# Reordering the end of a hybrid decoder layer on eight Trainium2 cores: two interleaved column blocks, x added from SBUF with plain stores, and weight buffers freed head by head

## The chip, the cores and the metric

The kernel runs on the eight NeuronCores of one Trainium2 chip. Each core computes 2048 of the 16384 tokens, and no core talks to another. The metric is device time in microseconds of the slowest core. A program on all eight cores has two states: in some executions a few cores get a lower TensorE clock and the time is some per cent longer, whatever the kernel.

Engine names in the profile: PE is TensorE (matmuls), DVE is VectorE, ACT is ScalarE, POOL is GpSimd, SP is the sync engine. A trailing q (SPq, POOLq) is that engine's instruction queue.

## The reference, cut to what matters

Only the last step is touched by the change. y is the concatenation of three mixer branches A, B and C, 1024 channels each, already multiplied by its gates:

```python
g_a, g_b, g_c = split_cols(branch_norm[l], BRANCH_WIDTHS)
y = jnp.concatenate([rmsnorm(ya, g_a), rmsnorm(yb, g_b), rmsnorm(yc, g_c)], axis=-1)
out = jnp.einsum('bse,ed->bsd', y, w_out[l])      # (tokens x 3072) @ (3072 x 2048)
x = x + rmsnorm(out, norm_post[l])
```

## The kernel before: the parts that matter

y lies transposed in SBUF (channels on partitions), and w_out comes in 12 pieces of 1 MB in bfloat16 on arrival: four column blocks `db` of 512 columns times three branches `br`. The kernel has five buffers for these pieces and nine for finished rows, and does the 16 token tiles in two groups (`half`, 7 and 9 tiles), so all of w_out is read twice. For each tile, column block and branch, eight matmuls fill one PSUM bank (a "group" below, 1.71 us). ScalarE evicts branch 0, scaled by the branch's root-mean-square; VectorE adds branches 1 and 2; ScalarE squares the sum.

```python
def o_evict(half, db, i, br):
    ...
    if br == 0:    # ScalarE
        P.op("act", lambda e: e.activation(out=ra, in_=pv, func=AF.Identity, scale=sc(c)), ...)
    else:          # VectorE
        P.op("dve", lambda e: e.scalar_tensor_tensor(out=ra, in0=pv, scalar=sc(c), in1=ra, op0=ALU.mult, op1=ALU.add), ...)
    if br == 2:    # ScalarE: sum of squares of this column block
        P.op("act", lambda e: e.activation(out=asrow(i, psb(b)), in_=ra, func=AF.Square, accum_out=...), ...)
```

When all four column blocks of a tile are there, `final` multiplies the row and adds it to `out`, which already holds a copy of x (made by DMA much earlier). The addition is done by an accumulating DMA:

```python
def final(half, i):
    ...                                     # reduce_sum (DVE), sqrt (ACT), reciprocal (DVE)
    P.op("dve", lambda e: e.scalar_tensor_tensor(out=rf, in0=rf, scalar=sc(ST_FR + t), in1=asrow(i, gpost[:]),
                                                 op0=ALU.mult, op1=ALU.mult), ...)          # 128 x 2048
    P.op("pool", lambda e: e.dma_start(out=asrow(i, out_d[t * 128:(t + 1) * 128, :]), in_=rf,
                                       accum_op=ALU.add), reads=Mr, waits=xcp, dma_sem=f"d_out{i}")
```

The order of work: in each column block the first two and last two tiles go branch by branch, the tiles between them one after the other. The weight piece that comes five pieces later is loaded when the last tiles have used its buffer. Buffers 0 to 3 lie where the weights of branch B lay, so the first pieces wait for branch B. Tile rows of the second group reuse the SBUF of the first group's rows, and so must wait until those have been stored.

```python
for half in range(2):
    n = NT[half]                            # 7, 9
    for db in range(4):
        head, mid, tail = [0, 1], list(range(2, n - 2)), [n - 2, n - 1]
        ...                                 # head: by branch; mid: tile by tile; tail: by branch, load_wo(1) after each branch
        if db == 3: ...                     # final of a tile one unit after its last group, the last three at the end
```

## Time and profile before

| | before |
|---|---|
| time of the fast runs | 1366.8, 1367.25, 1367.4 us |
| PE busy, share of the span | 1243.3 us, 91% |
| last matmul to end of the program, core 0 | 36.8 us |
| PE waits in the output projection, core 0 | 1.9 (pool engine) + 4.7 (weights) + 7.1 us (weights) |

First the page of the kernel before: the span, and two rows of its 40 equal slices of 34 us each. A digit is the busy share of the slice in tenths (9 is 90% or more).

```profile
span 1366.8 us, 17431 instructions; the slowest of 8 cores (1359.3 to 1366.8 us)
PE   2686799999999999999999999999899997999990
DMA  9921129741299990303003411303254499825198
```

PE is full except at the beginning, which the change leaves alone, in slices 29 and 34, and in the last one.

The waits of PE from 960 us on (total, number of times, longest):

```profile
PE ps L364 <- DMA arena<-wst: 11.8, 2, 7.1
PE ps L510 <- POOL arena L503: 1.9, 1, 1.9
```

And the tail in the timeline (start, duration, engine, line, operation; in brackets the idle time before it and what ended that):

```profile
1319.69 10.31 PE L364 MATMUL ps<-arena 128*128 128x512 bf16 x47
1330.11 0.75 DVE L932 SCALAR_TENSOR_TENSOR arena<-ps,arena 128x512 f32<-128x512 f32 x1 [0.97 <-PE ps L364]
1332.28 2.35 DVE L950 SCALAR_TENSOR_TENSOR arena<-arena 128x2048 f32<-128x2048 f32 x1
1335.46 2.35 DVE L950 SCALAR_TENSOR_TENSOR arena<-arena 128x2048 f32<-128x2048 f32 x1
1338.63 2.35 DVE L950 SCALAR_TENSOR_TENSOR arena<-arena 128x2048 f32<-128x2048 f32 x1
1342.12 1.44 POOL L953 DMA_DIRECT2D out<-arena  x1 [1.85 <-issue]
```

L932 is the last eviction, 0.9 us after the last matmul. L950 is the multiply of `final`: three are left, one after the other. The last accumulating store is issued at 1342.1, but the program ends only at 1366.8: the stores issued earlier are still in the queue ahead of it.

### The profile page before, as it was taken

The page shows a single profiled execution, that of the slowest core. Times are in us where ns is not written, and L with a number is a line of the kernel's source. Part 1 is how long each engine was busy: PE and PEld are TensorE (multiplying, and loading weights), DVE is VectorE, ACT ScalarE, POOL GpSimd, SP SyncE. Part 2 cuts the span into 40 slices and gives each one's busy share as a digit, 9 for nine tenths or more (in the row PEclk, how much of TensorE's full clock was granted, in tenths as well). Part 3 has the DMA queues.
Part 4 walks back from the last instruction along what each step waited for, and adds up shares of the span by engine and source line. Part 5 has one row for each costly group of instructions (what it writes and reads, how often), then busy time and mean ns, then how long its engine had stood idle before and what let it go on. Part 6 is the DMA issues. An engine that isn't in the chain of part 4 may idle for free.

```text
span 1366.8 us, 17431 instructions; the slowest of 8 cores (1359.3 to 1366.8 us)
## 1 busy us (share of the span) xinstructions
PE 1243.3 (91%) x6242; PEld 575.8 (42%) x6242; DVE 533.5 (39%) x868; ACT 431.2 (32%) x781; POOL 126.4 (9%) x165
## 2 busy tenths in 40 slices
PE   2686799999999999999999999999899997999990
PEld 0232345544444444444444444444434443444440
DVE  3646564435544433443222223322322254223362
ACT  2254332122245555553322222222222222222220
POOL 1000021110101010101001010101100011000011
PEclk7798899999999999999999999999999999999995
DMA  9921129741299990303003411303254499825198
GB/s 243 252 81 62 62 43 168 122 67 34 32 182 158 166 166 9 63 1 62 1 0 50 75 28 35 63 1 62 53 85 82 89 153 154 137 50 93 32 152 125
DMA packets 25284, 119.38 MB, mean 87 GB/s; under 512 B 2672, under 2 KB 4976, under 8 KB 20720
## 3 DMA queue, kind: packets, MB, share of 16 engines
q0 software_dynamic: 21136, 80.22, 36.2%
q1 hardware_dynamic: 4064, 38.05, 11.9%
q8 instruction: 51, 0.84, 0.3%
q14 instruction: 33, 0.27, 0.1%
HBM read 164.93 MB, written 33.55 MB: 145 GB/s over the span
## 4 chain that ended last, share of the span: by engine, by line
PE 82%; DVE 6%; DMA 5%; ACT 2%; issue 2%; POOL 0%; DVEq 0%; SPq 0%; ACTq 0%; POOLq 0%
PE ps L364 81%; DMA arena<-wst 3%; DVE arena L439 2%; DMA arena<-xT 2%; DVE arena L420 1%; ACT arena L430 1%; DVE arena L950 1%; DVE arena L531 1%; DVE arena L473 1%; PE ps L700 1%; PE ps L510 0%; DVE arena L537 0%; ACT arena L499 0%; ACT arena L464 0%; DVE arena L577 0%
## 5 line engine op out<-in xcount | busy, mean ns | idle before, releaser
L364 PE MATMUL ps<-arena 128*128 128x512 bf16 (+3 forms) x5922 | 1236.9, 370 | 79.1 <-ACT arena L430 53.6
L364 PEld LDWEIGHTS ps<-arena 128*128 128x128 bf16 x5922 | 561.6, 98 | 730.9 <-issue 122.5
L496 ACT ACTIVATE arena<-arena 128x512 bf16<-128x512 f32 x96 | 68.8, 716 | 398.2 <-DVE arena L839 173.2
L932 DVE SCALAR_TENSOR_TENSOR arena<-ps,arena 128x512 f32<-128x512 f32 x128 | 95.9, 751 | 201.0 <-PE ps L364 181.1
L503 POOL TENSOR_TENSOR arena<-arena 128x512 bf16<-128x512 bf16 x48 | 55.1, 1148 | 730.2 <-ACT arena L499 636.4
L936 ACT ACTIVATE ps<-arena 128x512 f32<-128x512 f32 x64 | 38.5, 601 | 223.8 <-DVE arena L932 186.2
L531 DVE TENSOR_TENSOR arena<-arena 128x512 f32<-128x512 f32 (+5 forms) x80 | 64.3, 803 | 77.7 <-ACT arena L525 72.7
L371 POOL DMA_DIRECT2D arena<-wst x96 | 56.5, 607 | 393.1 <-PE ps L364 375.8
L833 DVE SCALAR_TENSOR_TENSOR arena<-ps,arena 128x512 f32<-128x512 f32 x32 | 24.1, 752 | 154.7 <-PE ps L364 83.3
L647 DVE CAST arena<-ps 128x512 bf16<-128x512 f32 x32 | 22.1, 692 | 101.6 <-PE ps L364 98.8
L499 ACT ACTIVATE arena<-arena 128x512 bf16<-128x512 f32 x96 | 58.8, 613 | 0.0
L929 ACT ACTIVATE arena<-ps,arena 128x512 f32<-128x512 f32 x64 | 43.3, 683 | 25.4 <-PE ps L364 11.7
L776 DVE BATCH_NORM_STATS2 arena<-ps 128x6 f32<-128x512 f32 x32 | 22.4, 699 | 73.0 <-PE ps L364 70.2
L517 ACT ACTIVATE arena<-ps 128x512 f32<-128x512 f32 x64 | 36.3, 596 | 40.0 <-PE ps L364 39.6
L439 DVE SCALAR_TENSOR_TENSOR arena<-arena 128x512 bf16<-128x512 f32 x64 | 42.8, 745 | 0.4
L420 DVE RECIPROCAL arena<-arena 128x512 f32<-128x512 f32 (+2 forms) x6 | 15.4, 2570 | 67.3 <-ACT arena L418 43.5
L950 DVE SCALAR_TENSOR_TENSOR arena<-arena 128x2048 f32<-128x2048 f32 x16 | 37.6, 2351 | 1.7
L525 ACT COPY arena<-ps 128x512 f32<-128x512 f32 x32 | 18.5, 578 | 60.0 <-PE ps L510 53.5
L430 ACT ACTIVATE arena<-arena 128x2048 bf16<-128x2048 f32 x16 | 30.0, 1905 | 8.4 <-DMA arena<-xT 7.5
L675 ACT ACTIVATE ps<-ps,arena 128x256 f32<-128x256 f32 x64 | 28.5, 446 | 3.1
L793 ACT ACTIVATE arena<-ps,arena 128x512 bf16<-128x512 f32 x32 | 23.1, 773 | 10.7 <-DVE arena L788 10.0
L517 ACT ACT_TABLE_LOAD x20 | 25.7, 1283 | 0.4
(55 smaller groups left out, 364.5 us busy)
## 6 DMA issues: line engine op xcount, KB each, us to landing
arena<-wst POOLq DMA_DIRECT2D x72, 512.0 KB, 13.6
arena<-wst POOLq DMA_DIRECT2D x24, 1024.0 KB, 13.6
arena<-xT SPq DMA_DIRECT2D x16, 1024.0 KB, 11.9
out<-arena POOLq DMA_DIRECT2D x16, 1024.0 KB, 14.2
arena<-memT SPq DMA_DIRECT2D x2, 1024.0 KB, 6.2
arena<-norm_post SPq DMA_DIRECT2D x1, 1024.0 KB, 4.8
arena<-poolw_l POOLq DMA_DIRECT2D x1, 512.0 KB, 30.6
arena<-sguw_l SPq DMA_DIRECT2D x1, 512.0 KB, 10.7
```

The lines of the kernel that those rows point to most:

```text
L364: return lambda e: e.matmul(out, lhsT=lhsT, rhs=rhs, start=start, stop=stop)
L371: return P.op("pool", lambda e: e.dma_start(out=out, in_=in_), reads, writes, waits, dma_sem=sem)
L430: P.op("act", lambda e, i=i, si=si: e.activation(out=sqx[si][:], in_=xp[i % 6][:].rearrange("p k t -> p (k t)"), func=AF.Square), reads=[M ...
L439: P.op("dve", lambda e, i=i, k=k: e.scalar_tensor_tensor(out=hT[:, k, tb * 512:(tb + 1) * 512], in0=xp[i % 6][:, k % 4, :], scalar=cp[:, C ...
L496: P.op("act", lambda e: e.activation(out=yT[:, c, tb * 512:(tb + 1) * 512], in_=tmp[ti][:], func=AF.Copy, scale=cp[:, CP_GBR + c:CP_GBR + ...
L499: P.op("act", lambda e: e.activation(out=sq[si][:], in_=tmp[ti][:], func=AF.Square), reads=[M_tmp[ti]], writes=[M_sq[si]])
L503: P.op("pool", lambda e: e.tensor_tensor(out=sqp[:], in0=sq[0][:], in1=sq[1][:], op=ALU.add), reads=[M_sq[0], M_sq[1]], writes=[M_sqp])
L517: P.op("act", lambda e: e.activation(out=tmp[ti][:], in_=psb(b), func=AF.Silu), reads=[bk(b)], writes=[M_tmp[ti]])
L531: P.op("dve", lambda e, cur=cur, dst=dst, lo=lo, sh=sh: e.tensor_tensor(out=dst[:, lo:528], in0=cur[:, lo:528], in1=cur[:, lo - sh:528 - s ...
L929: P.op("act", lambda e: e.activation(out=ra, in_=pv, func=AF.Identity, scale=sc(c)), reads=[bk(b), "rbr"], writes=[row_M(i, db)])
L932: P.op("dve", lambda e: e.scalar_tensor_tensor(out=ra, in0=pv, scalar=sc(c), in1=ra, op0=ALU.mult, op1=ALU.add), reads=[bk(b), "rbr", row_ ...
L950: P.op("dve", lambda e: e.scalar_tensor_tensor(out=rf, in0=rf, scalar=sc(ST_FR + t), in1=asrow(i, gpost[:]), op0=ALU.mult, op1=ALU.mult), ...
```

## The change

The intent is to shorten the tail and to remove the weight waits:

1. The last two column blocks of the second group are interleaved, so that tiles finish every two units (10.4 us) rather than every unit (5.2 us).
2. The last four tiles do not use the accumulating store. Their row is multiplied by norm_post on the pool engine block by block, their x row is loaded into the row buffer of a tile that is already stored, VectorE does row * scale + x, and a plain store from the sync engine writes it. The last tile is stored in four parts.
3. The last group of branch B runs head by head, so the first head's weight buffers come free 28 us earlier. The first column block runs all seven tiles by branch. A sixth weight buffer is opened in y, and each weight piece is loaded in two halves.
4. The second group starts with rows that the first group did not use. Less visible: the finals of the first group come one tile later than before.

```diff
-    wo = [at(f"wo{i}", o_wo[i], [128, 8, 512], BF16) for i in range(5)]
+    wo = [at(f"wo{i}", o_wo[i], [128, 8, 512], BF16) for i in range(5)] + [yT[:, 16:24, 0:512]]
+    o_slot = [i % 5 for i in range(12)] + [2, 3, 4, 0, 1, 5, 2, 3, 4, 0, 1, 5]
 ...
+    for hl in range(2):                      # branch B, last group: head by head
+        for tb in range(4):
+            b_unit(3, hl, tb, tb % 2)
+            flush()
+            single_ss(1, tb, tb % 2, hl == 1)   # sums of squares per head, no pair sum on the pool engine
+        load_wo(1)
     load_wo(1)
 ...
+            if xadd:                         # last four tiles
+                P.op("pool", lambda e: e.tensor_tensor(out=ra, in0=ra, in1=gpost[:, db * 512:(db + 1) * 512],
+                                                       op=ALU.mult), ...)
 ...
+    def final_x(i, parts):
+        ...
+                P.op("dve", lambda e, av=av, xr=xr: e.scalar_tensor_tensor(
+                    out=av, in0=av, scalar=sc(ST_FR + t), in1=xr, op0=ALU.mult, op1=ALU.add), ...)
+            dma_sp(out_d[...], rows[i][...], reads=ms, sem=f"d_ox{i}{p}")
 ...
+    by_branch(0, 0, list(range(7)), True)
+    for db in range(1, 4):
+        by_branch(0, db, [0, 1], False)
+        for i in range(2, 5):
+            unit(0, db, i)
+            if db == 3:
+                final(0, i - 2)
+        by_branch(0, db, [5, 6], True)
+        if db == 3:
+            for i in range(3, 7):
+                final(0, i)
 ...                                          # second group, blocks 0 and 1 as before
+    seq = [(0, 2), (1, 2), (2, 2), (3, 2), (0, 3), (4, 2), (1, 3), (5, 2), (2, 3), (6, 2), (3, 3), (7, 2),
+           (4, 3), (8, 2), (5, 3), (6, 3), (7, 3), (8, 3)]       # (position of the tile, column block)
+    pend = []
+    for p, db in seq:
+        i = ordr[p]
+        unit(1, db, i)
+        for q in pend:
+            if q < 5:
+                final(1, ordr[q])
+            else:
+                final_x(ordr[q], 1)
+            if q < 4:
+                load_xrow(ordr[q + 5], ordr[q])
+        pend = [p] if db == 3 else []
+    final_x(ordr[8], 4)
```

More of the change, by code (lines that the diff above doesn't have):

```diff
@@ L500, in finish_y, with single_ss, f @@
              reads=[M_tmp[ti]], writes=[M_sq[si]])
+    def single_ss(br, tb, si, last):
+        def f():
+            fns = []
+            for q in range(4):
+                col = br * 16 + tb * 4 + q
+                fns.append(lambda e, col=col, q=q: e.matmul(
+                    ps[:, 0, col:col + 1], lhsT=sq[si][:, q * 128:(q + 1) * 128], rhs=ones[:, 0:1],
+                    start=False, stop=last, skip_group_check=True))
+            P.group("pe", fns, reads=[M_sq[si], "ones"], writes=[bk(0)])
+        late.append(f)
     def pair_ss(br, tb, first, last):
@@ L819, in build_program, with b_unit @@
     load_group(("B", 1))
-    def b_unit(j, hl, tb):
+    def b_unit(j, hl, tb, ti):
         h = 2 * j + hl
@@ L831, in b_unit @@
                        for q in range(4)], reads=[M_vh(h, tb * 4, 4), M_ws], writes=[bk(bz)])
-        ti = hl
         P.op("dve", lambda e: e.scalar_tensor_tensor(
@@ L840, in b_unit @@
              reads=[bk(bg), M_tmp[ti]], writes=[M_tmp[ti]])
-        finish_y(8 + h, tb, ti, hl)
+        finish_y(8 + h, tb, ti, ti)
     stream = [(half, db, br) for half in range(2) for db in range(4) for br in range(3)]
+    o_slot = [i % 5 for i in range(12)] + [2, 3, 4, 0, 1, 5, 2, 3, 4, 0, 1, 5]
     onext = [0]
@@ L852, in load_wo, with M_wo, copy_x @@
             half, db, br = stream[i]
-            s = i % 5
-            c = CH[("O", db, br, 0)]
-            dst = wo[s][:].rearrange("p (c k) n -> p c (k n)", c=2)
-            src = w_d[c:c + 2].rearrange("c p n -> p c n")
-            dma_pool(dst, src, writes=[Mem((o_wo[s], 8 * KB))], sem=f"d_o{s}")
-    xcp = []
-    for j in range(4):
-        if j < 3:
-            for tb in range(4):
-                b_unit(j, 0, tb)
-                flush()
-                b_unit(j, 1, tb)
-                pair_ss(1, tb, j == 0, j == 3)
-            if j < 2:
-                load_group(("B", j + 2))
-            else:
-                load_wo(2)
-        else:
-            for tb in range(4):
-                b_unit(j, 0, tb)
-                flush()
-                b_unit(j, 1, tb)
-                pair_ss(1, tb, j == 0, j == 3)
-        xcp.append(dma_sp(out_d[j * 512:(j + 1) * 512, :], x_d[j * 512:(j + 1) * 512, :], sem=f"d_xc{j}"))
+            s = o_slot[i]
+            for hf in range(2):
+                c = CH[("O", db, br, hf)]
+                dma_pool(wo[s][:, hf * 4:hf * 4 + 4, :], w_d[c].rearrange("p (k n) -> p k n", k=4),
+                         writes=[M_wo(s, hf)], sem=f"d_o{s}{hf}")
+    def M_wo(s, hf):
+        if s < 5:
+            return Mem((o_wo[s] + hf * 4 * KB, 4 * KB))
+        return Mem(*[(YA + (16 + hf * 4 + k) * 4 * KB, KB) for k in range(4)])
+    XC = [(0, 7), (7, 10), (14, 16)]
+    xcp = {}
+    def copy_x(n):
+        lo, hi = XC[n]
+        tok = dma_sp(out_d[lo * 128:hi * 128, :], x_d[lo * 128:hi * 128, :], sem=f"d_xc{n}")
+        for t in range(lo, hi):
+            xcp[t] = tok
+    for j in range(3):
+        for tb in range(4):
+            b_unit(j, 0, tb, 0)
+            flush()
+            b_unit(j, 1, tb, 1)
+            pair_ss(1, tb, j == 0, j == 3)
+        if j < 2:
+            load_group(("B", j + 2))
+        else:
+            load_wo(2)
+        copy_x(j)
+    for hl in range(2):
+        for tb in range(4):
+            b_unit(3, hl, tb, tb % 2)
+            flush()
+            single_ss(1, tb, tb % 2, hl == 1)
+        load_wo(1)
     load_wo(1)
@@ L886, in branch_rstd, with tok_of @@
         P.op("dve", lambda e: e.reciprocal(out=sc(ST_RBR, 48), in_=sc(ST_RBR, 48)), reads=["rbr"], writes=["rbr"])
-    NT = [7, 9]
+    ordr = [7, 8, 0, 1, 2, 3, 4, 5, 6]
+    T1 = {i: 7 + i for i in range(9)}
+    def tok_of(half, i):
+        return i if half == 0 else T1[i]
     def row_ap(i, db):
@@ L912, in o_mm @@
     def o_mm(half, db, i, br):
-        t = i if half == 0 else 7 + i
-        n = half * 12 + db * 3 + br
-        s = n % 5
+        t = tok_of(half, i)
+        s = o_slot[half * 12 + db * 3 + br]
         b = bank()
         obank[(i, br)] = b
-        P.group("pe", [mm(psb(b), yT[:, br * 8 + k, t * 128:(t + 1) * 128], wo[s][:, k, :], k == 0, k == 7)
-                       for k in range(8)],
-                reads=[M_ytile(br * 8, t), Mem((o_wo[s], 8 * KB))], writes=[bk(b)])
+        for hf in range(2):
+            ks = range(hf * 4, hf * 4 + 4)
+            P.group("pe", [mm(psb(b), yT[:, br * 8 + k, t * 128:(t + 1) * 128], wo[s][:, k, :], k == 0, k == 7)
+                           for k in ks],
+                    reads=[M_ytile(br * 8, t), M_wo(s, hf)], writes=[bk(b)])
     def o_evict(half, db, i, br):
-        t = i if half == 0 else 7 + i
+        t = tok_of(half, i)
+        xadd = half == 1 and i in ordr[5:]
         b = obank[(i, br)]
@@ L938, in o_evict, with final_rstd @@
                  reads=[row_M(i, db)], writes=[bk(b), ("so", t, db)])
-    def final(half, i):
-        t = i if half == 0 else 7 + i
+            if xadd:
+                P.op("pool", lambda e: e.tensor_tensor(out=ra, in0=ra, in1=gpost[:, db * 512:(db + 1) * 512],
+                                                       op=ALU.mult),
+                     reads=[row_M(i, db), M_gp], writes=[row_M(i, db)])
+    M_gp = Mem((H + 56 * KB, 8 * KB))
+    def final_rstd(t):
         P.op("dve", lambda e: e.reduce_sum(out=sc(ST_FO + t), in_=sc(ST_SO + t * 4, 4), axis=AX.X),
@@ L947, in final @@
              writes=[("fr", t)])
+    def final(half, i):
+        t = tok_of(half, i)
+        final_rstd(t)
         rf = row_full(i)
@@ L951, in final @@
                                                      op0=ALU.mult, op1=ALU.mult),
-             reads=[("fr", t), Mem((H + 56 * KB, 8 * KB))] + Mr, writes=Mr)
+             reads=[("fr", t), M_gp] + Mr, writes=Mr)
         P.op("pool", lambda e: e.dma_start(out=asrow(i, out_d[t * 128:(t + 1) * 128, :]), in_=rf,
                                            accum_op=ALU.add),
-             reads=Mr, waits=xcp, dma_sem=f"d_out{i}")
-    def ev(half, db, i, br):
-        o_evict(half, db, i, br)
-    for half in range(2):
-        n = NT[half]
-        for db in range(4):
-            head = list(range(2))
-            tail = list(range(n - 2, n))
-            mid = list(range(2, n - 2))
-            for grp in (head, mid, tail):
-                if grp is mid:
-                    for i in mid:
-                        for br in range(3):
-                            o_mm(half, db, i, br)
-                            ev(half, db, i, br) if (half, db) != (0, 0) or i > 1 else None
-                        if db == 3 and i >= 1:
-                            final(half, i - 1)
-                else:
-                    for br in range(3):
-                        for i in grp:
-                            o_mm(half, db, i, br)
-                        if half == 0 and db == 0 and grp is head and br == 0:
-                            branch_rstd()
-                            dma_sp(gpost[:], npost_d.partition_broadcast(128), writes=[Mem((H + 56 * KB, 8 * KB))],
-                                   sem="d_c3")
-                        for i in grp:
-                            ev(half, db, i, br)
-                        if grp is tail:
-                            load_wo(1)
-                    if db == 3:
-                        if grp is head:
-                            final(half, 0)
-                        else:
-                            final(half, n - 3)
-                            final(half, n - 2)
-                            final(half, n - 1)
-            if half == 0 and db == 0:
-                load_wo(2)
@@ new lines, in final, with load_xrow @@
+             reads=Mr, waits=[xcp[t]], dma_sem=f"d_out{i}")
+    xrow = {}
+    def load_xrow(i, j):
+        t = tok_of(1, i)
+        xrow[i] = j
+        dma_sp(row_full(j), asrow(j, x_d[t * 128:(t + 1) * 128, :]),
+               writes=[row_M(j, db) for db in range(4)], sem=f"d_xr{j}")
+    def final_x(i, parts):
+        t = tok_of(1, i)
+        j = xrow[i]
+        final_rstd(t)
+        w = 4 // parts
+        for p in range(parts):
+            dbs = range(p * w, p * w + w)
+            for db0 in dbs if j >= 7 else dbs[:1]:
+                nd = 1 if j >= 7 else w
+                a = rows[i][:, db0:db0 + nd, :].rearrange("p a b -> p (a b)")
+                xr = row_ap(j, db0) if j >= 7 else rows[j][:, db0:db0 + nd, :].rearrange("p a b -> p (a b)")
+                av = a.rearrange("p (a b) -> p a b", b=256) if j >= 7 else a
+                ms = [row_M(i, db) for db in range(db0, db0 + nd)]
+                P.op("dve", lambda e, av=av, xr=xr: e.scalar_tensor_tensor(
+                    out=av, in0=av, scalar=sc(ST_FR + t), in1=xr, op0=ALU.mult, op1=ALU.add),
+                    reads=[("fr", t)] + ms + [row_M(j, db) for db in range(db0, db0 + nd)], writes=ms)
+            ms = [row_M(i, db) for db in dbs]
+            dma_sp(out_d[t * 128:(t + 1) * 128, dbs[0] * 512:dbs[-1] * 512 + 512],
+                   rows[i][:, dbs[0]:dbs[-1] + 1, :].rearrange("p a b -> p (a b)"), reads=ms, sem=f"d_ox{i}{p}")
@@ new lines, in unit, with by_branch @@
+    def unit(half, db, i):
+        for br in range(3):
+            o_mm(half, db, i, br)
+            o_evict(half, db, i, br)
+    def by_branch(half, db, grp, last):
+        for br in range(3):
+            for i in grp:
+                o_mm(half, db, i, br)
+            if half == 0 and db == 0 and br == 0:
+                branch_rstd()
+                dma_sp(gpost[:], npost_d.partition_broadcast(128), writes=[M_gp], sem="d_c3")
+            for i in grp:
+                o_evict(half, db, i, br)
+            if last:
+                load_wo(1)
+                if half == 0 and db == 3 and br == 2:
+                    load_wo(1)
@@ new lines, in build_program @@
+    by_branch(0, 0, list(range(7)), True)
[9 more added lines that the diff above has]
+                final(0, i)
+    for db in range(2):
+        by_branch(1, db, ordr[:2], False)
+        for i in ordr[2:7]:
+            unit(1, db, i)
+        by_branch(1, db, ordr[7:], True)
@@ new lines, in build_program @@
+    seq = [(0, 2), (1, 2), (2, 2), (3, 2), (0, 3), (4, 2), (1, 3), (5, 2), (2, 3), (6, 2), (3, 3), (7, 2),
[3 more added lines that the diff above has]
+        i = ordr[p]
+        unit(1, db, i)
+        for q in pend:
[6 more added lines that the diff above has]
+        pend = [p] if db == 3 else []
```

## The prediction

> **What bounds the kernel now.** TensorE: the page gives PE busy 1243 of 1366.8 us (91%), and the chain of waits has PE on 82% of it. The change touches only the last third. There the timeline and the waits of core 0 show three losses:
> 1. Start of the output projection: PE waits 1.95 us for the pool engine's pair sum, then 4.74 us for weights (to 994.1; other cores wait 2.8 to 7.4 us for those weights).
> 2. Between the two token groups: 7.1 us for weights (to 1148.5; up to 11 us on other cores), queued behind four accumulating stores.
> 3. The tail: the last matmul ends at 1330.0, the span at 1366.8: 36.8 us. Three 2.35 us multiplies run one after another, and six accumulating 1 MB stores (issued every 5.4 us from 1299, served in 6 to 6.5 us) have piled up; the last two go in 1 KB pieces.
>
> **Costs, step by step (estimates from those durations).**
> - Start: the weights come 28 us early by head order, and seven tiles run by branch. New price: all seven PSUM banks are taken before the branch statistics exist, so PE waits once for sum, square root with table load and first eviction (983.9 to 987.1 in the trace, 3.3 us), plus 16 more tiny matmuls (about 1 us). Saves 2 to 5 us.
> - Between groups: one accumulating store fewer is ahead of the weights, but DMA was nearly keeping up, so this saves only about 1.5 us of wait 2. Then comes a new wait. Behind the first weight load, the queue holds three more loads (before: two) and four row stores (before: three). ScalarE waits before show rows landing at 1171.9, 1177.9, 1182.8: 6 us each; from 1148.5 to 1171.9 two loads and a store: about 8.7 us a load. So row 6 lands near 1147.5 + 3*8.6 + 4*6 = 1197. It is needed at the ninth tile of the second group: its first-branch matmuls start at 1172.1 without stalls, and seven banks let PE run 7*1.7 us more, to 1184. PE thus loses about 14 us there instead of 7. Net loss 7.
> - Tail: last eviction, square, root (2.3 us), one 2048-wide multiply (2.35), root again (0.8), four 512-wide multiplies (0.75 each) end 8.4 us after PE. Plain stores of the last two tiles, 8 KB packets at about 0.4 us over 16 engines, are done near 11.5; the span closes 4.8 us after the last packet, as before. About 16.5 us instead of 36.8: saves 20. The interleaving makes finals 10 us apart, so accumulating stores keep up. The Trainium skill, "DMA: Bandwidth & Descriptors", section "SWDGE vs HWDGE vs iDMA", says accumulation must be issued from GpSimd while plain stores can go from Sync, as the trace's queues agree. The pool multiplies (16, about 1.2 us) are off the path.
>
> **Sum.** 1367.4 - 3 + 7 - 20 = about 1351 us, 1.2% faster. Range 1338 to 1362. Faster by over 2%: 0.2; within 2%: 0.79; slower: 0.01.
>
> **What would show each step.** Tail from last matmul to end 15 to 19 us. At the start no weight wait, one 3.3 us PE gap. Between groups: PE waits 4 to 6 us for weights, and about 8 us more, in pieces, for evictions that wait on row stores ("DMA out<-arena"), up to 12 us each on ScalarE. No PE wait in the interleaved blocks.
>
> **What would make it wrong.** If rows land sooner (less contention among the eight cores), the between-groups loss vanishes and the gain is over 2%. If plain stores contend with leftover accumulating stores, the tail stays above 20 us. If VectorE and pool hold each other up in the last tiles, or four final multiplies in a row delay evictions, PE stalls more.

## More of the kernel before

DMA is full around slice 34 and in slices 39 and 40. So DMA hardly matters on the average and matters a great deal at two places. The share of busy time in four stretches says the same (view of windows, core 0; the columns are the stretch, its length, busy time and instructions of PE, weight loads, DVE, ACT and POOL, granted clock, DMA share, GB/s):

```profile
1115.00:1180.00 65.00, 57.89 (x261) 25.67 (x260) 29.49 (x37) 14.85 (x36) 7.41 (x9) 0.95 1.02 161
1180.00:1230.00 50.00, 50.00 (x233) 22.69 (x232) 15.44 (x21) 15.33 (x34) 2.20 (x3) 1.00 0.39 65
1330.00:1367.00 37.00, 0.00 (x0) 0.00 (x0) 8.49 (x10) 1.50 (x6) 3.71 (x3) 0.54 0.89 126
```

From 1115 to 1180 us, where the first group ends and the second begins, DMA is busy without a pause (1.02). In the last 37 us PE does nothing and DMA is at 0.89.

## The result, and the profile after

The changed kernel took 1347.7 and 1349.5 us in its two fast runs, and 1371.1 and 1371.6 us in two slow ones. The ratio to the kernel before is 0.9864 (95% interval 0.9835 to 0.9893): 1.4% faster, which is within 2%. A control gave 0.9870 (0.9851 to 0.9890). It was run at another time. Ratios here are the mean time of one kernel's fast runs over that of the other's of the same rounds, so not quite the ratio of the medians.

The page of the changed kernel, the rows as above:

```profile
span 1346.1 us, 17672 instructions; the slowest of 8 cores (1344.2 to 1346.1 us)
PE   2686799999999999999999999999999998999993
DMA  9921129743099922212100703214272559976295
```

The hole in slice 29 is gone, the one near slice 34 is still there, and the last slice of PE is partly filled. PE's waits from 960 us on, core 5:

```profile
PE ps L364 <- DMA arena<-wst: 6.1, 2, 3.9
PE ps L364 <- ACT arena L960: 6.0, 2, 3.2
```

L960 is the eviction of branch 0 on ScalarE (L929 before). The two waits on it are 3.2 us at the start of the projection, where all seven PSUM banks are full before the branch statistics exist, and 2.9 us between the groups. The two waits for weights, 3.9 and 2.2 us, are the two halves of one weight piece between the groups. (On cores 0, 2 and 4 the view puts the first of them, 4.2 to 4.3 us, down to a reduction on VectorE, L978. The last semaphore step of the weight half came 0.24 us before PE went on there, as on core 5, so it is counted as a wait for weights below.) The 2.9 us come from row stores, which the ScalarE timeline of core 5 shows (idle time and releaser in brackets; the four rows are the first that the second group takes over from tiles still being stored):

```profile
1166.39 0.69 ACT L960 ACTIVATE arena<-ps,arena 128x512 f32<-128x512 f32 x1 [4.51 <-DMA out<-arena]
1172.76 0.69 ACT L960 ACTIVATE arena<-ps,arena 128x512 f32<-128x512 f32 x1 [2.96 <-DMA out<-arena]
1180.69 0.69 ACT L960 ACTIVATE arena<-ps,arena 128x512 f32<-128x512 f32 x1 [4.53 <-DMA out<-arena]
1186.36 0.69 ACT L960 ACTIVATE arena<-ps,arena 128x512 f32<-128x512 f32 x1 [4.99 <-DMA out<-arena]
```

PE loses more here than the waits. From 1137.3 us on, just after the first wait for weights, core 5 was granted half the clock for 6.8 us (view of windows, PE alone: busy time, granted clock, DMA share, GB/s):

```profile
1137.34:1144.17 6.83, 4.66 (x12) 0.50 1.05 161
```

In the clock records of both kernels all eight cores have such a spell at 0.5 between the groups, after a first wait of 3.6 to 11.1 us: 6.8 to 13.7 us long in the kernel before, 6.8 to 10.2 us in the changed kernel. In e12 below, whose waits there are 2.7 us at most, seven of the eight cores have none.

The tail of core 5 in the timeline:

```profile
1317.77 5.99 PE L364 MATMUL ps<-arena 128*128 128x512 bf16 x27
1322.44 3.45 DVE L1021 SCALAR_TENSOR_TENSOR arena<-arena 128x512 f32<-128x512 f32 x4
1325.82 0.74 DVE L963 SCALAR_TENSOR_TENSOR arena<-ps,arena 128x512 f32<-128x512 f32 x1
1326.73 0.75 DVE L963 SCALAR_TENSOR_TENSOR arena<-ps,arena 128x512 f32<-128x512 f32 x1 [0.17 <-DVE arena L963]
1328.55 1.26 POOL L971 TENSOR_TENSOR arena<-arena 128x512 f32<-128x512 f32 x1 [5.20 <-ACT arena L980]
1328.97 2.99 DVE L1021 SCALAR_TENSOR_TENSOR arena<-arena 128x2048 f32<-128x2048 f32 x1 [0.17 <-DVE arena L982]
1332.79 2.74 DVE L1021 SCALAR_TENSOR_TENSOR arena<-arena 128x512 f32<-128x512 f32 x4
```

The last matmul ends at 1323.8. L1021 is the new multiply-and-add. VectorE is still busy with the final of the tile two before the end (1322.44 to 1325.89) when the last matmul ends, so the last two evictions (L963) end at 1327.5 instead of about 1324.7. Then comes the final of the last tile but one (2.99 us, while the pool engine multiplies), and only then that of the last tile. The last multiply ends 11.8 us after PE. In that window DMA is far from full now (share 0.40, against 0.89 in the tail before):

```profile
1323.80:1346.10 22.30, 0.00 (x0) 0.00 (x0) 9.69 (x15) 1.20 (x4) 1.26 (x1) 0.61 0.40 143
```

To compare whole kernels I use three figures, each the mean of the eight cores in the profiled run, worked out from the instruction times: the output projection (from the end of the last gating matmul of branch B to the last matmul), the time from the last matmul to the end of the last multiply, and the tail (last matmul to end of the program).

| run | ratio to before | output projection, us | last matmul to last multiply, us | tail, us |
|---|---|---|---|---|
| before | 1 | 353.0 | 11.0 | 36.2 |
| changed kernel | 0.9864 | 347.3 | 11.8 | 22.5 |
| changed kernel, control | 0.9870 | 349.0 | 11.8 | 22.3 |
| e1, accumulating stores for all | 0.9906 | 348.3 | 8.5 | 27.7 |
| e2, no interleaving | 0.9995 | 348.6 | 29.2 | 39.2 |
| e3, head order undone | 0.9854 | 347.5 | 11.5 | 21.5 |
| e4, last tile's blocks together | 0.9839 | 347.0 | 10.1 | 19.2 |
| e5, finals at once | 0.9827 | 349.2 | 8.6 | 17.4 |
| e6b, first weight early | 0.9875 | 349.4 | 11.8 | 22.0 |
| e7, rows before later weights | 0.9835 | 346.6 | 11.7 | 22.2 |
| e8, e6b and e7 | 0.9818 | 343.8 | 11.8 | 21.9 |
| e12, e8 and earlier finals | 0.9787 | 339.4 | 11.7 | 22.2 |
| e11, all of it | 0.9698 | 335.4 | 5.7 | 13.9 |

Two profiles of the same changed kernel differ by 1.8 us in the projection, so differences of that size in that column are not read as effects. The intervals of the ratios are about 0.0015 to 0.003 wide on each side.

### The profile page after: what moved, and what is told of

Its sections match the earlier page's. It is cut to its first block, busy times and chain, and to the rows that moved or that the text cites. A ratio compares the mean times of both kernels' runs of the same rounds, so it can differ in the third digit from the quotient of the medians.

```text
span 1346.1 us, 17672 instructions; the slowest of 8 cores (1344.2 to 1346.1 us)
## 1 busy us (share of the span) xinstructions
PE 1242.0 (92%) x6258; PEld 576.2 (43%) x6258; DVE 539.2 (40%) x877; ACT 430.5 (32%) x781; POOL 148.0 (11%) x197
## 4 chain that ended last, share of the span: by engine, by line
PE 82%; DMA 7%; DVE 6%; ACT 2%; issue 2%; DVEq 0%; SPq 0%; POOL 0%; ACTq 0%; POOLq 0%
PE ps L364 81%; DMA out<-arena 3%; DMA arena<-xT 2%; DVE arena L439 2%; ACT arena L430 1%; DMA arena<-wst 1%; DVE arena L420 1%; DVE arena L991 1%; DVE arena L473 1%; DVE arena L542 1%; PE ps L711 1%; DVE arena L1021 0%; PE ps L521 0%; ACT arena L464 0%; DVE arena L548 0%
## 5 line engine op out<-in xcount | busy, mean ns | idle before, releaser
L963 DVE SCALAR_TENSOR_TENSOR arena<-ps,arena 128x512 f32<-128x512 f32 x128 | 95.7, 750 | 186.0 <-PE ps L364 158.3
L514 POOL TENSOR_TENSOR arena<-arena 128x512 bf16<-128x512 bf16 x44 | 50.6, 1150 | 676.2 <-ACT arena L499 583.2
L371 POOL DMA_DIRECT2D arena<-wst x120 | 66.0, 566 | 313.9 <-PE ps L364 284.6
L960 ACT ACTIVATE arena<-ps,arena 128x512 f32<-128x512 f32 x64 | 42.9, 685 | 27.4 <-DMA out<-arena 17.0
L971 POOL TENSOR_TENSOR arena<-arena 128x512 f32<-128x512 f32 x16 | 20.2, 1262 | 109.8 <-ACT ps L967 75.7
L991 DVE SCALAR_TENSOR_TENSOR arena<-arena 128x2048 f32<-128x2048 f32 x12 | 31.1, 2590 | 1.2
## 6 DMA issues: line engine op xcount, KB each, us to landing
arena<-xT SPq DMA_DIRECT2D x16, 1024.0 KB, 11.8
out<-arena POOLq DMA_DIRECT2D x12, 1024.0 KB, 11.6
```

Source lines behind the costliest of these rows:

```text
L371: return P.op("pool", lambda e: e.dma_start(out=out, in_=in_), reads, writes, waits, dma_sem=sem)
L514: P.op("pool", lambda e: e.tensor_tensor(out=sqp[:], in0=sq[0][:], in1=sq[1][:], op=ALU.add), reads=[M_sq[0], M_sq[1]], writes=[M_sqp])
```

## The experiments

All are edits of the changed kernel. The first four ran in one call, the next four in a second, three in a third, the last alone; each call has its own runs of the kernel before (the calls fell on three chips).

### e1 and e2: which of the two parts of the tail does the work

```diff
# e1: interleaving kept, all nine tiles finish with the accumulating store (x copied to out for them all)
-        xadd = half == 1 and i in ordr[5:]
+        xadd = False
-            if q < 5: final(1, ordr[q])      else: final_x(ordr[q], 1)      (and load_xrow)
+            final(1, ordr[q])
# e2: plain stores kept, blocks 2 and 3 one after the other
-    seq = [(0, 2), (1, 2), ..., (8, 3)]
+    seq = [(p, 2) for p in range(9)] + [(p, 3) for p in range(9)]
```

> The changed kernel with the interleaved blocks kept, but all nine tiles of the second group finish as before (x copied to out, one 2048-wide multiply, accumulating store, no pool multiply). Theory A (the interleaving is what takes the backlog of stores away): the accumulating stores are at most two deep at the last matmul, so the time from last matmul to end is 24 to 27 us, only 2 to 5 us more than the 22.3 us of the changed kernel. Rival B (the plain stores do it): the tail goes back above 32 us. Also: if the pool multiplies slow the VectorE multiplies down, the 2048-wide ones return here from a mean of 2.59 us to 2.35 us.

> The changed kernel with plain stores for the last four tiles kept, but the last two column blocks one after the other (no interleaving). Theory A: finals come 5.2 us apart again while an accumulating store needs about 6.5 us and the x rows come on top, so the last x rows or stores are late: tail 25 to 32 us, 3 to 10 us worse than the changed kernel. Rival B (plain stores alone do it): tail 22 to 23 us, the same time as the changed kernel within 2 us.

Measured: e1 has a tail of 27.7 us, just above theory A's 24 to 27 and well below rival B's 32. Its time is 0.9906 of the kernel before. e2 is as slow as the kernel before (0.9995), with a tail of 39.2 us, worse than theory A had it. The waits of e2 show why, on its slowest core, in the view of waits and in the timeline:

```profile
DVE arena L1021 <- DMA arena<-x: 16.6, 1, 16.6
1337.11 2.74 DVE L1021 SCALAR_TENSOR_TENSOR arena<-arena 128x512 f32<-128x512 f32 x4 [16.63 <-DMA arena<-x]
```

An x row is loaded into the buffer of a tile whose accumulating store must land first. With finals every 5.2 us those stores pile up again (16.8 us from issue to landing at the median, 11.6 in the changed kernel), the x rows come late, and VectorE, which works in order, stands still for 16.6 us at the first of them, with the last evictions behind it. So the two parts do not add up. Both runs keep the changes at the start and between the groups (their projections are 4.4 to 4.7 us shorter than before), so the parts are compared in the tail alone, 36.2 us before: plain stores without interleaving make it 3.0 us longer, interleaving without plain stores takes off 8.5 of the 13.7 us, and plain stores on top of it another 5.2 us.

The other point of e1's expectation also holds. Without multiplies on the pool engine every 2048-wide multiply takes 2351 ns. First e1, then the changed kernel (groups by line; count, busy us, mean ns):

```profile
L991 DVE SCALAR_TENSOR_TENSOR arena<-arena 128x2048 f32<-128x2048 f32 x16 | 37.6, 2351 | 1.7
```

```profile
L991 DVE SCALAR_TENSOR_TENSOR arena<-arena 128x2048 f32<-128x2048 f32 x12 | 31.1, 2590 | 1.2
```

The Trainium skill, "SBUF — State Buffer", section "SBUF: two separate sides", says that VectorE instructions with two SBUF inputs and GpSimd instructions that read SBUF take turns at a shared port pair, for a whole instruction. The trace agrees: of the 2048-wide multiplies of the changed kernel, on all cores, those that start while a pool multiply runs take 2.99 to 3.08 us, the others 2.35.

### e3: is the head order needed

```diff
-    for hl in range(2):
-        for tb in range(4):
-            b_unit(3, hl, tb, tb % 2); flush(); single_ss(1, tb, tb % 2, hl == 1)
-        load_wo(1)
-    load_wo(1)
+    for tb in range(4):
+        b_unit(3, 0, tb, 0); flush(); b_unit(3, 1, tb, 1); pair_ss(1, tb, False, True)
+    load_wo(3)
```

> The changed kernel with only the head order of the last B group undone (both heads per token block, pair sums on the pool engine, three weight loads at the end), seven tiles by branch kept. Theory C (running seven tiles by branch already hides the weights, as the third weight is first needed 24 us later): no PE wait for weights at the start of the output projection, one gap of 3.2 us as in the changed kernel, and about 1 us less from the 16 tiny matmuls that go; total within 1 us or 1 us faster. Rival D (the early weights are needed): a weight wait of 3 to 7 us comes back there.

Measured: 0.9854, not different from the changed kernel within the intervals. On all eight cores no weight wait comes back at the start, and the one gap there is 3.2 us as in the changed kernel. So theory C holds: with seven tiles by branch the third weight piece is first needed after 14 groups (24 us), in the kernel before after 4 (6.8 us). The head order, which the change names, brings nothing that can be measured.

### e4 and e5: what sets the tail of 22.5 us

```diff
# e4: (8, 2) moved to just before (8, 3)
-           (4, 3), (8, 2), (5, 3), (6, 3), (7, 3), (8, 3)]
+           (4, 3), (5, 3), (6, 3), (7, 3), (8, 2), (8, 3)]
# e5: e4, and each final issued right after its own unit
         unit(1, db, i)
+        pend = [p] if db == 3 and p < 8 else []
         for q in pend: ...
-        pend = [p] if db == 3 else []
```

> The changed kernel with one unit moved: the third column block of the last tile is done just before its fourth, so that the finals of the tiles before it run while PE still works. Theory E (the tail is 22.3 us and not 16.5 because VectorE serves the finals of the two tiles before, 3.5 and 3.0 us, in front of the last evictions and the last tile's final): last eviction ends 0.9 us after the last matmul, four multiplies end at about 5.5 to 6 us instead of 11.8, tail 16 to 18 us, total 4 to 6 us less. Rival F (the stores' data or the end of the program set the tail): the tail falls by less than 2 us.

> The kernel of e4 (third block of the last tile moved to just before its fourth) with each final issued straight after its own unit instead of after the next one. Theory E2 (in e4 the finals follow each other every 6.45 us while a unit takes 5.2 us, because root and reciprocal of a tile wait on ScalarE behind the square of the next tile, so VectorE is three finals late at the last matmul): the finals of tiles six to eight are over before the last matmul, the last multiply ends 5.5 to 6.5 us after it (e4: 10.1; changed kernel: 11.8), tail 14.5 to 16 us, time 3.5 us below e4. Rival: VectorE then holds up the next evictions and PE loses as much as the tail gains, or the end of the program hides it: no gain over e4.

Measured: e4 takes 3.3 us off the tail, which is more than rival F allowed and less than theory E expected. The last multiply ends 10.1 us after the last matmul, not 6. In its timeline the finals of four successive units start at 1311.4, 1317.8, 1324.3 and 1330.8, so every 6.45 us, while PE needs 5.2 us a unit. VectorE falls behind by 1.3 us with each of them. e5 was to mend that and did not: the next finals come after 6.4 and 7.0 us, because VectorE now stands still itself while ScalarE does square and root (0.97 and 0.49 us of idle time in a row), and the projection is no shorter. The tail is 1.9 us shorter, the ratio 0.9827 against 0.9839, inside the intervals: the expected 3.5 us did not come. Theory E was right about the engine and incomplete about the reason: one tile after the other takes VectorE longer than PE takes for a unit. Of the 6.45 us in e4, 1.09 us are a wait for ScalarE's root and 3.45 us the multiply, which runs in four pieces and against a pool multiply; one undisturbed 2048-wide multiply takes 2.35 us. By these numbers either alone would nearly close the gap of 1.25 us. Which of them counts was not tested singly: e11 changes both.

### e6, e6b, e7, e8 and e12: the stretch between the groups

```diff
# e6/e6b: the first weight the second group waits for goes to the sixth buffer, loaded after tile 3 of block 3
-    o_slot = ... + [2, 3, 4, 0, 1, 5, 2, 3, 4, 0, 1, 5]
+    o_slot = ... + [2, 3, 5, 0, 1, 4, 2, 3, 5, 0, 1, 4]
             unit(0, db, i)
+            if db == 3 and i == 3: load_wo(1)
# e7: the three weights needed only for block 1 of the second group are loaded after the row stores
             for i in range(3, 7): final(0, i)
+            load_wo(3)                       # and taken out of by_branch there
# e8: both
# e12: e8, and the finals of the first group one tile earlier, as in the kernel before
+        if db == 3: final(0, 0)              # after the first two tiles
-                final(0, i - 2)
+                final(0, i - 1)
```

> The changed kernel with two weight buffers swapped, so that the weight the second group waits for (its third-branch one) is loaded after the fourth tile of the last block, before two of the three accumulating stores. Theory G (the DMA queue bounds the stretch between the groups as a whole): the PE wait for weights of about 6 us goes to 0, but the row stores land when they did, so the PE wait for ScalarE evictions behind row stores grows from 1 to 3 us to 7 to 10 us: total the same within 2 us. Rival H (the two waits are separate): total 5 to 6 us less.

> The changed kernel with the three weight loads that are needed only 40 us later moved behind the four row stores. Theory G (row stores wait in the queue behind these loads): ScalarE no longer waits for row stores (now 11 to 17 us in sum), the second PE wait (1 to 3 us) goes, the weight wait of about 6 us stays; 2 to 4 us less. If the loads are then late, a PE wait of up to 5 us for weights appears at the second block of the group.

> e6 and e7 together. Theory G: both PE waits between the groups go to 0 and the time falls by 7 to 10 us against the changed kernel, though e6 alone gives nearly nothing and e7 alone 2 to 4 us. Rival H: the sum of what e6 and e7 gave singly.

> e6 mended: in e6 one weight load stood in the program ahead of the matmuls that still read its buffer, which gave a wrong result and a wait of 26 us. Here only the first weight of the second group is loaded early; the other loads stay where the changed kernel has them. Theory G (the queue bounds the whole stretch): the first weight wait (about 6 us) goes, the PE wait for evictions behind row stores grows to 6 to 9 us, total within 2 us of the changed kernel (0.985 to 0.988 of the kernel before). Rival H: 5 to 6 us less than the changed kernel.

> e8 (first weight early, row stores ahead of the later weights) and, new, the finals of the first group one tile earlier, as the kernel before had them, so that the chain of stores and loads starts about 5 us sooner. Theory G2 (in e8 the DMA queue is busy without a pause from the first store to the last load, and that load is about 5 us late whatever the order): the PE waits for weights at the second block (5 to 6.5 us in sum in e8) fall below 1.5 us, and the time falls 4 to 5 us below e8, 7 to 9 us below the changed kernel. Rival: the queue is not the bound, the waits stay.

e6 is a mistake and says nothing about the theories: one load stood in the program ahead of matmuls that still read the old content of its buffer. The result was wrong (relative error 0.14) and PE waited 26 us for that load.

e6b, the mended version, is the clearest test. None of its cores has a PE wait for weights any more, and on the slowest the waits for row stores have grown by more than that:

```profile
ACT arena L960 <- DMA out<-arena: 27.3, 4, 14.9
PE ps L364 <- ACT arena L960: 14.2, 4, 5.3
```

Of the 14.2 us, 3.2 belong to the start; so 11 us stand where 9 us stood (6.1 + 2.9). Over the eight cores it is 6.2 to 12.4 us, 8.9 in the mean, against 7.8. The time is that of the changed kernel (0.9875). Theory G holds, rival H falls: the wait moved from the weights to the row stores. e7 takes the row-store waits away on all eight cores and leaves about 7 us of weight wait. Its 0.9835 is about 4 us less than the changed kernel, but the intervals overlap (0.9820 to 0.9850 against 0.9835 to 0.9893), and PE's waits in the stretch fall only from 7.8 to 7.0 us, so a gain from e7 alone is not shown. e8 gives 0.9818, by the ratios 6 us less than the changed kernel (3.5 and 5.2 us in the projection against its two profiles) and less than the 7 to 10 expected. Its slowest core:

```profile
PE ps L364 <- DMA arena<-wst: 6.3, 4, 2.2
PE ps L364 <- ACT arena L960: 3.2, 1, 3.2
```

These weight waits are new ones, at the second block of the group: the loads that were put behind the row stores now come late. Whatever goes first, the last transfer of the stretch is late, since the queue has no pause in it (the DMA share from 1126 to 1190 us is 1.03 in the changed kernel and in e8). e12 lets the chain of transfers start a tile earlier. It reaches 0.9787, 4.2 us below e8 by the ratios (0.0031 of 1367), as expected, and 10.5 us below the changed kernel, where 7 to 9 were expected. The weight waits fall to 1.7 to 3.2 us on the eight cores (mean 2.6, 5.3 in e8), not quite to the 1.5 expected. That is less than the 4.4 us by which the projection is shorter; much of the rest lies in the clock. The spells at 0.5 between the groups add up to 7.7 us a core in the changed kernel, 3.0 in e8 and 0.4 in e12 (2.6 us less at half the clock are about 1.3 us, an estimate). The slowest core of e12 has the full clock there (its window, columns as in the first such view):

```profile
1126.00:1190.00 64.00, 60.80 (x281) 27.17 (x280) 25.05 (x33) 17.47 (x41) 14.47 (x19) 1.00 1.03 159
```

The Trainium skill, "DMA: Bandwidth & Descriptors", section "Two DMAs through the same engine are not ordered", states that within one queue of one DMA engine descriptors start in order but are pipelined, so that the end of a later one does not tell that an earlier one's write is done. In this trace the transfers of GpSimd's queue between the groups landed in order of issue: on core 5 of the changed kernel the stores issued by 1120.8 had landed at 1132.3, the loads issued after them at 1159.4, and the four stores after those between 1166.3 and 1186.2.

### The control and e11: a version that beats both

e11 is e12 with five more edits: the start by branch in three and four tiles (the statistics are then ready before the banks run out); block 2 of the last tile just before its block 3, with three units of lead for block 2 in place of four; sum and root of a tile's final placed ahead of the last eviction of the next unit, its reciprocal and multiply after it; one 2048-wide instruction where the row layout had led to four; and the waits for the last stores put last among the waits at the end.

```diff
-    by_branch(0, 0, list(range(7)), True)
+    by_branch(0, 0, [0, 1, 2], False)
+    by_branch(0, 0, [3, 4, 5, 6], True)
 ...
+    seq = [(0, 2), (1, 2), (2, 2), (0, 3), (3, 2), (1, 3), (4, 2), (2, 3), (5, 2), (3, 3), (6, 2), (4, 3),
+           (7, 2), (5, 3), (6, 3), (7, 3), (8, 2), (8, 3)]
     for p, db in seq:
         i = ordr[p]
-        unit(1, db, i)
+        for br in range(3):
+            o_mm(1, db, i, br)
+            o_evict(1, db, i, br)
+            if br == 1:
+                for q in pend: final_rstd(tok_of(1, ordr[q]), True)   # sum (DVE) and root (ACT) only
         for q in pend: ...                                            # reciprocal, multiply, store
-        toks = sorted(self.count.items())
+        toks = sorted(self.count.items(), key=lambda kv: (kv[0].startswith("d_o"), kv[0]))
```

> The changed kernel unaltered, as control for the runs of this call and of the others. Expected: about 0.985 of the kernel before, tail near 22.5 us, PE waits of about 3.2 us at the start, 6 us for weights and 1 to 3 us for row stores.

> e12, and: three tiles by branch, then four, at the start (so that the statistics are ready before the PSUM banks run out; the 3.2 us gap should go); the last tile's third block just before its fourth; the sum and root of a tile's final issued before the last eviction of the next unit and its multiply after it, one 2048-wide multiply in place of four (VectorE then needs about 4.8 us a unit, under the 5.2 us of PE); and the waits at the end ordered so that those on the last stores come last. Expected: last multiply 5.5 to 6.5 us after the last matmul (11.8 in the changed kernel), tail 13 to 15 us, no PE wait above 1.5 us in the output projection; 15 to 19 us below the changed kernel, 0.972 to 0.975 of the kernel before.

Measured: the control took 0.9870. e11 took 1328.6 to 1329.9 us, 0.9698 of the kernel before (0.9684 to 0.9713), and gives the right result. That is 3.0% faster than the kernel before and 1.7% faster than the changed one, a little more than expected. The last multiply ends 5.7 us after the last matmul on every core, the tail is 13.9 us. PE's only waits on core 0 in the projection are these; the 2.3 us are more than the 1.5 expected:

```profile
PE ps L364 <- DMA arena<-wst: 2.6, 2, 2.3
```

Its VectorE in the last units (timeline, core 0), and below that the pool multiply (group by line):

```profile
1306.46 0.75 DVE L963 SCALAR_TENSOR_TENSOR arena<-ps,arena 128x512 f32<-128x512 f32 x1
1308.18 0.75 DVE L963 SCALAR_TENSOR_TENSOR arena<-ps,arena 128x512 f32<-128x512 f32 x1 [0.91 <-PE ps L364]
1309.18 2.35 DVE L1031 SCALAR_TENSOR_TENSOR arena<-arena 128x2048 f32<-128x2048 f32 x1 [0.17 <-DVE arena L986]
1311.64 0.75 DVE L963 SCALAR_TENSOR_TENSOR arena<-ps,arena 128x512 f32<-128x512 f32 x1
1313.37 0.75 DVE L963 SCALAR_TENSOR_TENSOR arena<-ps,arena 128x512 f32<-128x512 f32 x1 [0.97 <-PE ps L364]
1316.00 2.98 DVE L1031 SCALAR_TENSOR_TENSOR arena<-arena 128x512 f32<-128x512 f32 x4
```

```profile
L971 POOL TENSOR_TENSOR arena<-arena 128x512 f32<-128x512 f32 x16 | 28.0, 1750 | 98.1 <-ACT ps L967 98.1
```

Now VectorE waits for PE (0.91 and 0.97 us) instead of the last evictions waiting behind a final, and a unit's evictions come every 5.2 us. The multiply is back at 2.35 us and starts before the pool multiply, which takes 1.75 us at the mean (1.26 in the changed kernel): the loser of the port is now the engine that has time. e11 does not separate its five edits from each other; the start and the tail are separate in time and are read off separately in the table above (projection 4.0 us below e12, tail 8.3 us), but inside the tail the order of units, the place of the root, the single instruction and the order of the last waits were not run one by one.

## Why the prediction was right or wrong

The time was right: 1351 predicted, about 1349 measured (0.9864 of 1367.3), with the class "within 2%" at 0.79. But it was right by luck, as a sum of two wrong terms with opposite signs. The terms, with the mean of the eight cores where a core is not named:

| term | predicted, us | measured, us |
|---|---|---|
| start of the projection | 2 to 5 less, one gap of 3.3 | 6.7 of PE waits before, one gap of 3.2 after: 3.5 less |
| between the groups, PE waits | 14 instead of 7: 7 more | 7.8 instead of 9.3: 1.5 less |
| tail | 16.5 instead of 36.8: 20 less | 22.5 instead of 36.2: 13.7 less |
| sum | 16 less | 18.7 less |

**Start: right**, in mechanism and size. The prediction gave the head order a share of the credit ("the weights come 28 us early by head order, and seven tiles run by branch"); e3 shows that the seven tiles by branch do it alone.

**Between the groups: the mechanism was right, the size was not.** The new wait on row stores exists, in pieces of 3 to 5 us on ScalarE, and e7 shows that it is due to the weight loads ahead in the queue. But it cost PE 1.2 to 2.9 us and not the "about 8 us more" of the prediction. The mis-sized term is "about 8.7 us a load". I got it from the stretch 1148.5 to 1171.9 of the kernel before by taking 6 us for the one store in it; by the semaphores the store took 7.8 us there and the two loads 7.1 and 8.6. Measured in the changed kernel, three loads and a store take 26.8 us from the landing of the first weight to that of the first row (1139.6 to 1166.4), and rows land 6.7 us apart, so a load takes 6.7 us too. That makes the last row about 3 us earlier relative to the weights (46.7 us after them instead of 3 x 8.6 + 4 x 6 = 49.8). A further 2 to 3 us lie in PE, which took 44.7 us for its 196 matmuls from the weights to the point where it ran out of banks; at 1.71 us for eight these are 42. The prediction left out the clock: 4.5 us of the spell at 0.5 fall into this time and cost about 2.3 us (half of them, an estimate). Also, the 7 us of wait before were those of core 0; the mean over the cores was 9.3. What the prediction did not say is the more useful statement, shown by e6b: in this stretch the queue is the bound, and removing one of the two waits only moves it to the other.

**Tail: the direction was right, the size too hopeful.** The step that failed is "four 512-wide multiplies end 8.4 us after PE": it was 11.8. The sum started from an eviction 0.9 us after the last matmul and left out that VectorE was still at the final of an earlier tile, 3.45 us long, across the last matmul. The last evictions ended 3.7 us after it (1327.5 against 1323.8). The chance of this was named under "what would make it wrong", as VectorE and the pool engine holding each other up, but the larger part is lateness: 6.45 us a tile on VectorE against 5.2 us on PE, as e4's timeline shows. The port accounts for 0.64 us or a little more of each multiply that it hits and is part of the 6.45; how much of the rest is the wait for the root and how much the four pieces was not separated. From the last multiply to the end it was 10.7 us (22.5 - 11.8) and not 8.1 (16.5 - 8.4). The last packets of data moved on the average 4.6 us after the last multiply, where 3.1 were predicted, and the rest of the program took 6.1 us and not 4.8. Every engine closes with an instruction DRAIN, and GpSimd's ends last; the program is over 0.2 us after it, on every core. It takes 3.91 us in the kernel before and 5.54 us in the changed one (view of one source line: count, shortest, median and longest time in ns, first and last start):

```profile
L1000 POOLq DRAIN  x1: 3912/3912/3912, 1362.7 to 1362.7; - x1
L1083 POOLq DRAIN  x1: 5541/5541/5541, 1340.3 to 1340.3; - x1
```

So "the span closes 4.8 us after the last packet, as before" failed by a DRAIN that is 1.6 us longer. It is 5.54 us on all cores of every run that has the pool multiplies, and 3.83 us in e1, which has neither them nor the plain stores of results; which of the two lengthens it was not tested.

**"The interleaving ... so accumulating stores keep up": right**, and e1 and e2 show how much hangs on it. "The pool multiplies are off the path" was wrong by the port.

## What to carry to other kernels

Where a queue of transfers is full for a stretch, find the whole stretch and its last deadline before moving a single wait: making one transfer earlier moved the wait here, and starting the chain earlier, with the order changed, took most of it away (7.8 to 2.6 us). Look at the granted clock there too, for it was at half for some us after the longer waits. At the end of a kernel compare the time that the slowest in-order engine needs per tile, waits between its links included, with the time of a tile on the engine that feeds it; when it is longer, issuing everything sooner may not help (e5); shortening the multiply and putting the next tile's work between the links did here (e11, not separated). And two parts of a change that look independent should be tried apart, for here one of them was worth nothing without the other.

## What the Trainium skill lacked or had wrong

- No page gives the rate of an accumulating store. "DMA: Bandwidth & Descriptors" says that accumulation is issued from GpSimd, and gives no rate for it. Here 1 MB stores with accumulation landed 5.7 to 8.1 us apart when the queue was full on eight cores, 6.8 in the mean of the last nine of the kernel before, while plain 1 MB stores from the sync engine took 4.4 us from issue to landing at the median.
- "SBUF — State Buffer" is right about the shared port pair, but gives no such case: a 128x2048 multiply with two SBUF inputs takes 2.99 to 3.08 us instead of 2.35 when a 1.26 us pool multiply started first, and the pool multiply takes 2.35 to 2.65 us when VectorE started first.
- No page was found that gives the price of passing semaphores that are already reached; "Advanced Engine Details and Errata" has a figure for reading a semaphore's value only. In the changed kernel's end (core 5) TensorE passes one every 0.106 us, GpSimd every 0.061 and the sync engine every 0.050 us. The 17 waits after the last store's landing take about 1.8 us on TensorE, but nothing waits for them: they are over at 1341.5, and GpSimd's DRAIN ends at 1345.9. Ten of them on GpSimd put off the start of its DRAIN by 0.6 us; ordering them first was part of e11 and was not measured alone.
- After TensorE's last wait the program needed another 4.5 us in the changed kernel and 3.0 us in the kernel before. The runs show that GpSimd's closing DRAIN (5.54 and 3.91 us) fills that time; no page was found that says why it is longer in the one than in the other.
